# Hybrid RWKV-7 and attention layer: 64-byte buffer lines, score start tied to q and k, and a reordered recurrent build

## Chip, cores and metric

The program runs on one core of a Trainium2 chip. The metric is the device time of one execution in microseconds (us), given as the median of three runs; a profile of one execution goes with it. The engines are TensorE (PE, with its weight loads as PEld), VectorE (DVE), ScalarE (ACT), GpSimd (POOL) and SyncE (SP), which here only issues DMAs.

## What is computed

One layer on 512 tokens of width 2048 in fp32, with 16 attention heads and 16 RWKV-7 heads of 64 columns each:

```python
h = rms_norm(x, norm_g)
q, k, v, z_att, u_shift, z_rwkv = split(h @ w_in)     # one combined projection
att = dilated_mixture_attention(q, k, v, pos) * silu(z_att)
rwk = rwkv7_time_mix(u_shift, z_rwkv, ...)            # token shift, loras, recurrence, group norm, gate
x = x + concat([att, rwk]) @ w_out
return rms_norm(x, final_g)
```

The recurrence runs over the 512 tokens with a 64x64 state per head: `state = state*w + (state@a) b^T + v k^T`, `y = state @ r`. Attention is causal, and mixes three dilations by their softmax denominators.

## The kernel before

**Tiling.** Activations lie with 128 features on the partitions and 512 tokens along the free axis. A weight chunk is loaded as `raw` (512 KB), split by ScalarE and VectorE into a high and a low fp32r part (`whi`, `wlo`), and each product is made of three fp32r matmuls (`hh` with `whi`, `hl` with `whi`, `hh` with `wlo`). One output tile of the input projection takes 48 matmuls of 512 columns into a PSUM tile `mm_*` of pool `pm`. `run_main` writes this main stream tile by tile: `lora`, then `k`, `r`, `v` of the eight RWKV head pairs with the attention gates `z0` to `z7` between them, `gl128`, `qk00` to `qk33` (four groups g of four heads; a group has two head pairs, so pair = 2g or 2g+1), `v` of the attention, the RWKV gates `z8` to `z15`, and at the end the output projection (`mo`, `mh`, `mt`).

**Order.** The program is scheduled by hand. Everything that is not the main stream is a generator (`pre`, `subst`, `merges`, `build`, `scan` of the recurrent part; `assemble`, `att` of the attention; `gate_g`). After each matmul `pump()` resumes those whose turn has come by a small cost model (`Model`, `Engine`, `Tensor`, `Queue`): a `yield 0.1, t` says "resume 0.1 us after tile t is ready by the model". So a wait written in a generator moves where its instructions stand in every engine's queue; the engines themselves then work in order, and wait on semaphores for what they really need. The model knows reads and writes by tile name. It does not know when a buffer of a pool is taken over by a new tile: that wait is put in by the build.

**Pools.** `k2` has 20 buffers of up to 520 columns, `k4` has 9 of 1024 columns (four hold `vt` for the whole attention), `ps` in PSUM has 4. Tiles take them in turn.

**Attention.** `assemble(g, j, ...)` gathers q (j=0) and k (j=1) of a pair by eight DMAs each on SP (`qa_*`, `ka_*`, from the rotated tiles `m0_*`, `m2_*`), and makes `q`, `kd` and `kl` from them. `att(g)` runs over units (pair, block t of 128 queries): scores `s{pair}{head}{t}` (one matmul with `kd`, one with `kl`), masked maximum into `ss`, exp on ScalarE with its sum `den`; one unit later the transposes `pt` into `pa` (k4) and `pb` (k2); two units later, at t = 3, the product `po{pair}` with `vt`, and `yl{pair}` (the gate, fetched by DMA from `sp_s`) times `po`.

**RWKV gates.** `gate(idx, z_ps)` makes `zz`, `zt` (k2) and the gated `yl` from the main stream's tile; `gate_g(p)` makes `pg{p}` from `gh`, `gl`.

**Recurrent part.** `pre(p)` builds for pair p the operands of the blocked recurrence: `pM`, then `pb` (bonus), `L`, `FT` (from `pF`), `X`, `pQ`, and transposed blocks of `bt` and `v` into `X` and `A`. `L` is one buffer for all pairs, and so `pre(p)` waits there until pair p-1 is built.

Of the kernel before, what the change touches and what calls it, by code (L numbers as in the profile page):

```python
# [136 lines left out]
def hymba_kernel(ctx: ExitStack, tc: tile.TileContext, xT, x, wa, wb, wo, pv, w2a2, g2, fg,  # L137
# [20 lines left out]
    K1N, K2N, K4N, RAWN, AHEAD = 5, 20, 9, 2, 2  # L158

    def k2(shape, name, dt=F32):  # L160
        return kp.tile(shape, dt, tag="k2", bufs=K2N, name=name)

    def k1(shape, name, dt=F32):
        return kp.tile(shape, dt, tag="k1", bufs=K1N, name=name)
# [1 line left out]
    def k4(shape, name, dt=F32):  # L166
        return kp.tile(shape, dt, tag="k4", bufs=K4N, name=name)

    def ps(name, shape=(P, 512)):
        return pp.tile(list(shape), F32, tag="ps", name=name)  # L170

    def small(shape, name, bufs=12, dt=F32):
        return sp.tile(shape, dt, tag=f"s{shape[1]}", bufs=4 if shape[1] == 4 else bufs, name=name)

    pvt = cp.tile([P, NPV], F32, name="pvt")
    nc.scalar.dma_start(pvt, pv)

    def col(n, i):
        return pvt[:, PV[n] + i:PV[n] + i + 1]
# [7 lines left out]
    ones = k2([P, P], "ones")  # L187
    V.memset(ones, 1.0)
    bonesr = cp.tile([P, P], F32R, name="bonesr")
    hw0 = cp.tile([P, 16], F32, name="hw0")  # L190
    nka = cp.tile([P, 8], F32, name="nka")
    omu = cp.tile([P, 27], F32, name="omu")
    V.tensor_scalar(omu, pvt[:, 0:27], -1.0, 1.0, ALU.mult, ALU.add)
    warm = cp.tile([P, 1], F32, name="warm")
    S.activation(warm, ones[:, 0:1], AF.Tanh)

    hth, htl, normed = [], [], []
    rstd = cp.tile([P, T], F32, name="rstd")
    rtok = cp.tile([P, 4], F32, name="rtok")
    xt_b, xq_b, Lb = [], [], []  # L200

    def prologue():
# [52 lines left out]
    def later():  # L255
        bones = k2([P, P], "bones")
        Q.dma_start(bones, cst[:, 576:704])
        Q.dma_start(bmt, bmask)
        yield 1.59, bones
        V.tensor_copy(bonesr, bones)  # L260
        V.tensor_scalar(hw0, pvt[:, PV["w0"]:PV["w0"] + 16], 0.5, None, ALU.mult)
        V.tensor_scalar(nka, pvt[:, PV["k_a"]:PV["k_a"] + 8], -1.0, None, ALU.mult)
        for i in range(2):
            G.memset(xt_b[i], 0.0)
            G.tensor_copy(Lb[i][H[i], :, H[i]], ident[H[i], H[i]][:, None, :].to_broadcast([64, NCH, C]))
            yield 0.5, G
# [320 lines left out]
    def c3(t):  # L587
        return t.rearrange("p (c t) -> p c t", t=C)
# [38 lines left out]
    def pre(p, r, k, v):  # L627
# [80 lines left out]
        V.tensor_scalar(rn2, rn2, 1e-24, None, ALU.max)  # L708
        V.reciprocal(rn2, rn2)
        start(subst(p, Mp, rn2), 0.06, Mp, rn2, rank=-1)  # L710
        S.activation(a, a, AF.Identity, bias=nka[:, p:p + 1], scale=col("k_a", p))
        V.scalar_tensor_tensor(k, a, 1.0, k, ALU.add, ALU.mult)
        rk = k2([P, T], f"rk{p}")
        V.scalar_tensor_tensor(rk, r, col("r_k", p), k, ALU.mult, ALU.mult)
# [9 lines left out]
        V.tensor_tensor(bn, pb, v, ALU.mult)  # L724
        yield 0.1, bn
        spill_out(f"bn{p}", bn)
        while p >= 1 and p - 1 not in built:
            yield 0.5
        L = Lb
        X = [k4([P, NCH, P], f"X{h}_{p}") for h in range(2)]  # L730
        for h in range(2):
            S.copy(X[h][H[h], :, H[h]], ident[H[h], H[h]][:, None, :].to_broadcast([64, NCH, C]))
            evac(L[h][H[h], :, H[1 - h]], c3(k)[H[h]])
            evac(X[h][H[h], :, H[1 - h]], c3(r)[H[h]])
        yield 0.1, L[0], L[1]
        FT = k4([P, NCH, P], f"FT{p}")
        for q in range(2):
            pF = ps(f"pF{p}{q}", (P, 4, P))
            for c4 in range(4):
                c = 4 * q + c4  # L740
                for h in range(2):
                    TE.matmul(pF[H[h], c4, :], Fa[H[h], c, :], L[h][H[h], c, :], start=True, stop=True)
            V.tensor_tensor(FT[:, 4 * q:4 * q + 4, :], pF, fmask[:, None, :].to_broadcast([P, 4, P]), ALU.mult)
            yield 0.3
        yield 0.1, X[0], X[1]
        pQ = ps(f"pQ{p}", (P, NCH, C))
        for c in range(NCH):
# [8 lines left out]
        yield from blocks(lambda h: A[h], v, True, f"zv{p}")  # L756
        for h in range(2):
            G.memset(A[h][H[h], 0, :], 0.0)
        state[p] = dict(X=X, L=L, FT=FT, A=A, xt=xt_b[p % 2], wc=wc)
        yield 0.5  # L760

    def subst(p, Mp, rn2):
        V.tensor_tensor(Mp, Mp, rn2[:, None, :].to_broadcast([P, 32, 32]), ALU.mult)
# [266 lines left out]
    def att(g):  # L1030
        units = [(2 * g + pr_, t) for pr_ in range(2) for t in range(4)]
        po, ssb_, pts = {}, {}, {}
        for u in range(len(units) + 2):
            if u < len(units):
                pair, t = units[u]
                while pair not in ready or (t == 0 and u == 0 and pair >= 2 and pair - 1 not in scored):
                    yield 0.5
                tl_ = pairs[pair]
                n = max(256, 128 * (t + 1))
                nv = 128 * (t + 1)  # L1040
                tsl = slice(t * P, (t + 1) * P)
                for h in range(2):
                    sc = ps(f"s{pair}{h}{t}")
                    TE.matmul(sc[:, 0:n], tl_["q"][:, h, tsl], tl_["k", h][:, 0:n], start=True, stop=False)
                    TE.matmul(sc[:, 0:n], tl_["q"][:, h, tsl], tl_["kl", h][:, 0:n], start=False, stop=True)
                    ss = k2([P, T], f"ss{pair}{h}{t}")
                    nm = small([P, 1], f"nm{pair}{h}{t}")
                    V.tensor_tensor_reduce(ss[:, 0:nv], sc[:, 0:nv], att_mask(t), -0.125, 3.0e38,
                                           ALU.add, ALU.min, accum_out=nm)
                    den = small([P, 1], f"den{pair}{h}{t}")  # L1050
                    S.activation(ss[:, 0:nv], ss[:, 0:nv], AF.Exp, bias=nm, scale=-1.0, accum_out=den)
                    ssb_[u, h] = (ss, den)
                if t == 3:
                    scored.add(pair)
            if u >= 2:
                pair, t = units[u - 2]
                if t == 3:
                    po[pair] = pm.tile([P, T], F32, tag="mm", name=f"po{pair}")
                    for j in range(4):
                        for h in range(2):  # L1060
                            hd = (2 * pair + h) * 64
                            pa, pb = pts[pair, h]
                            pj = (pa[:, 0:512], pa[:, 512:896], pb[:, 0:256], pb[:, 256:384])[j]
                            TE.matmul(po[pair][H[h], j * P:T], vt[j][:, hd:hd + 64], pj,
                                      start=(j == 0), stop=(j == 3))
                if t == 3:
                    if f"s{pair}" in spill:
                        o = yl.pop(pair)
                        V.tensor_tensor(o, o, po.pop(pair), ALU.mult)
                    else:  # L1070
                        o = k2([P, T], f"o{pair}")
                        S.copy(o, po.pop(pair))
                    spill_out(f"o{pair}", o)
                elif t == 2 and f"s{pair}" in spill:
                    fetch_y(pair, f"s{pair}")
            if 1 <= u <= len(units):
                pair, t = units[u - 1]
                for h in range(2):
                    ss, den = ssb_.pop((u - 1, h))
                    if t == 0:  # L1080
                        pts[pair, h] = (k4([P, 1024], f"pa{pair}{h}"), k2([P, T], f"pb{pair}{h}"))
                    pa, pb = pts[pair, h]
                    pt = ps(f"pt{pair}{h}{t}")
                    for j in range(t + 1):
                        TE.transpose(pt[:, j * P:(j + 1) * P], ss[:, j * P:(j + 1) * P], ident)
                    if t == 0:
                        S.copy(pa[:, 0:P], pt[:, 0:P])
                    else:
                        S.copy(two(pa, t),
                               pt[:, 0:2 * P].rearrange("p (j c) -> p j c", j=2))  # L1090
                    if t >= 2:
                        S.copy(pb[:, (t - 2) * P:(2 * t - 3) * P], pt[:, 2 * P:(t + 1) * P])
            yield 0.0, S
            if u < len(units):
                for h in range(2):
                    ss, den = ssb_[u, h]
                    nv = 128 * (units[u][1] + 1)
                    V.reciprocal(den, den)
                    V.tensor_scalar(ss[:, 0:nv], ss[:, 0:nv], den, None, ALU.mult)
            yield 0.0, V  # L1100
# [324 lines left out]
```

## Time and profile before

| | |
|---|---|
| median of three runs | 1182.05 us (1180.76 to 1182.65) |
| the profiled execution | 1185.02 us |
| its span, first to last instruction | 1182.6 us |
| PE busy | 1149.7 us, 97% of the span |
| PEld busy | 941.8 us |
| DVE, ACT, POOL busy | 742.1, 560.8, 334.1 us |
| mean granted TensorE clock | 0.992 |
| DMA engines' mean busy share | 39.1% for the main queue |

PE is busy nearly all the time, so the time that PE stands idle, and the time in which its clock is at the lower level, is what work on the other engines can give back or cost. The rest of PE's time is matmuls.

### The profile page before, as it was taken

How to read it: one execution, taken by the hardware profiler on the slowest of the kernel's cores; microseconds unless marked ns; L12 is line 12 of the kernel's file. 1: busy time of each engine (PE TensorE's matmuls, PEld its weight loads, DVE VectorE, ACT ScalarE, POOL GpSimd, SP SyncE). 2: the span in 40 equal slices, each digit the busy share in tenths (PEclk: the TensorE clock that was granted, in tenths of full speed). 3: DMA queues.
4: the chain of work that ended last, by engine and by line, in shares of the span. 5: the costliest groups of instructions: out<-in, count | busy, mean ns of one | idle time of the engine just before them, and what ended most of it. 6: DMA issues, size and time to landing. Idle time of an engine off the chain costs nothing. (4 is left out here: it accounts for less than half of the span.)

```text
span 1182.6 us, 19112 instructions
## 1 busy us (share of the span) xinstructions
PE 1149.7 (97%) x6878; PEld 941.8 (80%) x6878; DVE 742.1 (63%) x1522; ACT 560.8 (47%) x1243; POOL 334.1 (28%) x586
## 2 busy tenths in 40 slices
PE   7999999999999999999999999999899999999997
PEld 5877778788778878787799978777777778888897
DVE  5767866868786778778653546465557657243252
ACT  6455444555746655555533345435354445222243
POOL 1005883635627174653640000101010000011020
PEclk9999999999999999999999999999999999999999
DMA  7333342334242424324242354433445336444343
GB/s 260 119 95 114 115 124 73 103 100 121 66 138 72 118 95 125 105 87 111 63 120 61 112 158 132 124 110 107 119 134 148 116 116 215 123 125 130 102 125 143
DMA packets 89870, 139.62 MB, mean 118 GB/s; under 512 B 37936, under 2 KB 47664, under 8 KB 89776
## 3 DMA queue, kind: packets, MB, share of 16 engines
q1 hardware_dynamic: 89344, 137.83, 39.1%
q8 instruction: 54, 0.88, 0.3%
q10 hardware_dynamic: 432, 0.58, 0.1%
q14 instruction: 40, 0.33, 0.1%
HBM read 114.44 MB, written 14.75 MB: 109 GB/s over the span
## 5 line engine op out<-in xcount | busy, mean ns | idle before, releaser
L88 POOL TENSOR_TENSOR Xtmp<-XT,Mp 128x248 f32<-128x248 f32 (+30 forms) x248 | 132.4, 534 | 168.5 <-DVE XT L88 151.1
L88 POOL TENSOR_TENSOR XT<-XT,Xtmp 128x248 f32<-128x248 f32 (+30 forms) x248 | 139.3, 562 | 21.7 <-DVE XT L88 2.1
L121 PE MATMUL mm_qk<-hh,whi 128*128 128x512 f32 x256 | 104.8, 410 | 0.8 <-ACT gtok L88 0.8
L121 PE MATMUL mm_qk<-hl,whi 128*128 128x512 f32 x256 | 104.2, 407 | 0.0
L121 PE MATMUL mm_qk<-hh,wlo 128*128 128x512 f32 x256 | 104.1, 407 | 0.0
L121 PE MATMUL mm_z<-hh,wlo 128*128 128x512 f32 x256 | 103.2, 403 | 0.0
L121 PE MATMUL mm_z<-hl,whi 128*128 128x512 f32 x256 | 103.2, 403 | 0.0
L88 DVE TENSOR_TENSOR wlo<-raw_o,whi 128x512 fp32r<-128x512 f32 x64 | 48.0, 792 | 87.3 <-ACT whi L88 87.3
L121 PE MATMUL mm_z<-hh,whi 128*128 128x512 f32 x256 | 102.7, 401 | 0.0
L88 POOL TENSOR_TENSOR y<-y,fg 128x512 f32<-128x512 f32 (+1 forms) x16 | 19.4, 1244 | 253.5 <-DMA raw_o<-in_wo_dram 156.7
L88 ACT ACTIVATE ss<-ss,nm 128x128 f32<-128x128 f32 (+3 forms) x64 | 35.6, 556 | 105.4 <-DVE nm L88 100.8
L88 ACT ACTIVATE whi<-raw_o 128x512 fp32r<-128x512 f32 x64 | 36.9, 623 | 96.3 <-PE mo L121 73.4
L88 POOL TENSOR_TENSOR m<-m,m 128x512 f32<-128x512 f32 x16 | 22.2, 1410 | 213.4 <-DVE m L88 127.7
L121 PE MATMUL mo<-whi,mh 128*128 128x512 f32 x192 | 75.8, 395 | 0.0
L121 PE MATMUL mo<-whi,ml 128*128 128x512 f32 x192 | 75.8, 395 | 0.0
L121 PE MATMUL mo<-wlo,mh 128*128 128x512 f32 x192 | 75.8, 395 | 0.0
L88 DVE TENSOR_TENSOR wlo<-raw_v,whi 128x352 fp32r<-128x352 f32 (+1 forms) x80 | 49.5, 640 | 33.8 <-ACT whi L88 33.0
L88 DVE TENSOR_TENSOR wlo<-raw_qk,whi 128x512 fp32r<-128x512 f32 x64 | 45.0, 716 | 31.8 <-ACT whi L88 31.7
L121 PE MATMUL mv<-whi,hh 128*128 128x352 f32 x192 | 62.5, 326 | 1.1 <-DVE m L88 1.1
L121 PE MATMUL mv<-whi,hl 128*128 128x352 f32 x192 | 62.4, 325 | 0.0
L121 PE MATMUL mv<-wlo,hh 128*128 128x352 f32 x192 | 62.3, 324 | 0.0
L88 ACT ACTIVATE whi<-raw_v 128x352 fp32r<-128x352 f32 (+1 forms) x80 | 41.3, 543 | 38.8 <-PE mv L121 25.8
(304 smaller groups left out, 3033.9 us busy)
## 6 DMA issues: line engine op xcount, KB each, us to landing
raw_z<-in_wa_dram SPq DMA_DIRECT2D x32, 512.0 KB
raw_qk<-in_wa_dram SPq DMA_DIRECT2D x32, 512.0 KB
raw_o<-in_wo_dram SPq DMA_DIRECT2D x32, 512.0 KB
raw_v<-in_wb_dram SPq DMA_DIRECT2D x24, 352.0 KB
raw_r<-in_wa_dram SPq DMA_DIRECT2D x16, 512.0 KB
raw_v<-in_wa_dram SPq DMA_DIRECT2D x16, 512.0 KB
raw_k<-in_wa_dram SPq DMA_DIRECT2D x15, 512.0 KB
xk<-in_xT_dram SPq DMA_DIRECT2D x16, 256.0 KB
```

Of the source, the lines that this page charges most:

```text
L88: return fn(o, *args, **kw)
L121: return fn(o, lhs, rhs, **kw)
```

## The change

Four things change. (1) Buffers: every `k2` tile is now a slice of a 528-column buffer (2112 bytes, a multiple of 64) instead of up to 520 columns (2080 bytes, which alternates between 0 and 32 past a 64-byte line); a few constant tiles are enlarged or merged (`nka` becomes columns 16 to 23 of `hw0`). (2) `att` waits at t = 0 by the model until `q` and both `kl` of the pair are written before it issues the pair's first scores. (3) In `pre`, `X`, `pQ` and the transposed blocks come first, and the wait for pair p-1 stands only ahead of `L` and `FT`. (4) `pre` ends with a wait for `FT` of 0.1 in place of a plain 0.5. No step of the arithmetic is changed.

```diff
--- before.py
+++ after.py
@@ -158,7 +158,9 @@
     K1N, K2N, K4N, RAWN, AHEAD = 5, 20, 9, 2, 2
 
     def k2(shape, name, dt=F32):
-        return kp.tile(shape, dt, tag="k2", bufs=K2N, name=name)
+        t = kp.tile([P, 528], dt, tag="k2", bufs=K2N, name=name)
+        t = t[:, 0:math.prod(shape[1:])]
+        return t if len(shape) == 2 else t.rearrange("p (a b) -> p a b", b=shape[2])
 
     def k1(shape, name, dt=F32):
         return kp.tile(shape, dt, tag="k1", bufs=K1N, name=name)
@@ -172,8 +174,8 @@
     def small(shape, name, bufs=12, dt=F32):
         return sp.tile(shape, dt, tag=f"s{shape[1]}", bufs=4 if shape[1] == 4 else bufs, name=name)
 
-    pvt = cp.tile([P, NPV], F32, name="pvt")
-    nc.scalar.dma_start(pvt, pv)
+    pvt = cp.tile([P, 112], F32, name="pvt")
+    nc.scalar.dma_start(pvt[:, 0:NPV], pv)
 
     def col(n, i):
         return pvt[:, PV[n] + i:PV[n] + i + 1]
@@ -187,16 +189,15 @@
     ones = k2([P, P], "ones")
     V.memset(ones, 1.0)
     bonesr = cp.tile([P, P], F32R, name="bonesr")
-    hw0 = cp.tile([P, 16], F32, name="hw0")
-    nka = cp.tile([P, 8], F32, name="nka")
+    hw0 = cp.tile([P, 32], F32, name="hw0")
     omu = cp.tile([P, 27], F32, name="omu")
     V.tensor_scalar(omu, pvt[:, 0:27], -1.0, 1.0, ALU.mult, ALU.add)
-    warm = cp.tile([P, 1], F32, name="warm")
+    warm = small([P, 1], "warm")
     S.activation(warm, ones[:, 0:1], AF.Tanh)
 
     hth, htl, normed = [], [], []
     rstd = cp.tile([P, T], F32, name="rstd")
-    rtok = cp.tile([P, 4], F32, name="rtok")
+    rtok = cp.tile([P, 16], F32, name="rtok")[:, 0:4]
     xt_b, xq_b, Lb = [], [], []
 
     def prologue():
@@ -258,8 +259,8 @@
         Q.dma_start(bmt, bmask)
         yield 1.59, bones
         V.tensor_copy(bonesr, bones)
-        V.tensor_scalar(hw0, pvt[:, PV["w0"]:PV["w0"] + 16], 0.5, None, ALU.mult)
-        V.tensor_scalar(nka, pvt[:, PV["k_a"]:PV["k_a"] + 8], -1.0, None, ALU.mult)
+        V.tensor_scalar(hw0[:, 0:16], pvt[:, PV["w0"]:PV["w0"] + 16], 0.5, None, ALU.mult)
+        V.tensor_scalar(hw0[:, 16:24], pvt[:, PV["k_a"]:PV["k_a"] + 8], -1.0, None, ALU.mult)
         for i in range(2):
             G.memset(xt_b[i], 0.0)
             G.tensor_copy(Lb[i][H[i], :, H[i]], ident[H[i], H[i]][:, None, :].to_broadcast([64, NCH, C]))
@@ -708,7 +709,7 @@
         V.tensor_scalar(rn2, rn2, 1e-24, None, ALU.max)
         V.reciprocal(rn2, rn2)
         start(subst(p, Mp, rn2), 0.06, Mp, rn2, rank=-1)
-        S.activation(a, a, AF.Identity, bias=nka[:, p:p + 1], scale=col("k_a", p))
+        S.activation(a, a, AF.Identity, bias=hw0[:, 16 + p:17 + p], scale=col("k_a", p))
         V.scalar_tensor_tensor(k, a, 1.0, k, ALU.add, ALU.mult)
         rk = k2([P, T], f"rk{p}")
         V.scalar_tensor_tensor(rk, r, col("r_k", p), k, ALU.mult, ALU.mult)
@@ -724,24 +725,10 @@
         V.tensor_tensor(bn, pb, v, ALU.mult)
         yield 0.1, bn
         spill_out(f"bn{p}", bn)
-        while p >= 1 and p - 1 not in built:
-            yield 0.5
-        L = Lb
         X = [k4([P, NCH, P], f"X{h}_{p}") for h in range(2)]
         for h in range(2):
             S.copy(X[h][H[h], :, H[h]], ident[H[h], H[h]][:, None, :].to_broadcast([64, NCH, C]))
-            evac(L[h][H[h], :, H[1 - h]], c3(k)[H[h]])
             evac(X[h][H[h], :, H[1 - h]], c3(r)[H[h]])
-        yield 0.1, L[0], L[1]
-        FT = k4([P, NCH, P], f"FT{p}")
-        for q in range(2):
-            pF = ps(f"pF{p}{q}", (P, 4, P))
-            for c4 in range(4):
-                c = 4 * q + c4
-                for h in range(2):
-                    TE.matmul(pF[H[h], c4, :], Fa[H[h], c, :], L[h][H[h], c, :], start=True, stop=True)
-            V.tensor_tensor(FT[:, 4 * q:4 * q + 4, :], pF, fmask[:, None, :].to_broadcast([P, 4, P]), ALU.mult)
-            yield 0.3
         yield 0.1, X[0], X[1]
         pQ = ps(f"pQ{p}", (P, NCH, C))
         for c in range(NCH):
@@ -756,8 +743,24 @@
         yield from blocks(lambda h: A[h], v, True, f"zv{p}")
         for h in range(2):
             G.memset(A[h][H[h], 0, :], 0.0)
+        while p >= 1 and p - 1 not in built:
+            yield 0.5
+        L = Lb
+        for h in range(2):
+            evac(L[h][H[h], :, H[1 - h]], c3(k)[H[h]])
+        yield 0.1, L[0], L[1]
+        FT = k4([P, NCH, P], f"FT{p}")
+        for q in range(2):
+            pF = ps(f"pF{p}{q}", (P, 4, P))
+            for c4 in range(4):
+                c = 4 * q + c4
+                for h in range(2):
+                    TE.matmul(pF[H[h], c4, :], Fa[H[h], c, :], L[h][H[h], c, :], start=True, stop=True)
+            V.tensor_tensor(FT[:, 4 * q:4 * q + 4, :], pF, fmask[:, None, :].to_broadcast([P, 4, P]), ALU.mult)
+            yield 0.3
         state[p] = dict(X=X, L=L, FT=FT, A=A, xt=xt_b[p % 2], wc=wc)
-        yield 0.5
+        yield 0.1, FT
+
 
     def subst(p, Mp, rn2):
         V.tensor_tensor(Mp, Mp, rn2[:, None, :].to_broadcast([P, 32, 32]), ALU.mult)
@@ -1036,6 +1039,8 @@
                 while pair not in ready or (t == 0 and u == 0 and pair >= 2 and pair - 1 not in scored):
                     yield 0.5
                 tl_ = pairs[pair]
+                if t == 0:
+                    yield 0.1, tl_["q"], tl_["kl", 0], tl_["kl", 1]
                 n = max(256, 128 * (t + 1))
                 nv = 128 * (t + 1)
                 tsl = slice(t * P, (t + 1) * P)
@@ -1171,7 +1176,7 @@
             yield 1.05
 
     fgt = []
-    ssq = cp.tile([P, 4, 5], F32, name="ssq")
+    ssq = cp.tile([P, 4, 8], F32, name="ssq")
     yt = {}
 
     def residual(nb):
```

The order of instructions shifts in the whole program from these waits. Three places, each with its queue before and after.

**VectorE at the start of pair 2** (first scores `s200`). Before, `kl_100` stands behind the product of `yl1` with `po1`:

```order
L88 TENSOR_TENSOR yl1_7964<-yl1_7964,po1_7994 128x512 [waits DMAHW6_49,PE_49,Pool_49]
L88 TENSOR_TENSOR m0_20_8012<-mm_qk20_7830,L0_234 128x512 [waits PE_49]
L88 TENSOR_TENSOR m3_20_8014<-mm_qk20_7830,L0_234 128x512
L88 TENSOR_TENSOR q_11_8016<-qa_110_7923,q_11_8016 64x512 [waits DMAHW1_49,DMAHW0_49,Activation_49]
L88 TENSOR_TENSOR q_11_8016<-qa_111_7928,q_11_8016 64x512 [waits DMAHW3_49,DMAHW2_49,Activation_49]
L88 TENSOR_TENSOR wlo112_8026<-raw112_qk22_7886,whi112_8025 128x512 [waits DMAHW5_49,Activation_49]
L88 TENSOR_TENSOR wlo112_8026<-raw112_qk22_7886,whi112_8025 128x512 [waits Activation_49]
L88 TENSOR_TENSOR kl_100_8047<-ka_100_7933,kd_100_8046 128x512 [waits DMAHW1_49,DMAHW7_49,DMAHW0_49,Activation_49]
L88 TENSOR_TENSOR kl_101_8051<-ka_101_7938,kd_101_8050 128x512 [waits DMAHW4_49,DMAHW3_49,DMAHW5_49,DMAHW2_49,Activation_49]
L88 ISA ss200_8062,nm200_8063<-s200_8059,L1_237 128x128 [waits PE_49]
```

After:

```order
L88 TENSOR_TENSOR kl_100_7976<-ka_100_7893,kd_100_7975 128x512 [waits DMAHW6_49,DMAHW1_49,DMAHW7_49,DMAHW0_49,Activation_49]
L88 TENSOR_TENSOR kl_101_7980<-ka_101_7898,kd_101_7979 128x512 [waits DMAHW4_49,DMAHW3_49,DMAHW5_49,DMAHW2_49,Activation_49]
L88 TENSOR_TENSOR m0_20_8001<-mm_qk20_7825,L0_233 128x512 [waits PE_49]
L88 TENSOR_TENSOR m3_20_8003<-mm_qk20_7825,L0_233 128x512 [waits PE_49]
L88 TENSOR_TENSOR wlo112_8010<-raw112_qk22_7881,whi112_8009 128x512 [waits Activation_49]
L88 TENSOR_TENSOR q_11_8032<-qa_110_7946,q_11_8032 64x512 [waits DMAHW1_49,DMAHW0_49,Activation_49]
L88 TENSOR_TENSOR q_11_8032<-qa_111_7951,q_11_8032 64x512 [waits DMAHW3_49,DMAHW2_49,Activation_49]
L88 TENSOR_TENSOR wlo112_8010<-raw112_qk22_7881,whi112_8009 128x512 [waits Activation_49]
L88 ISA ss200_8051,nm200_8052<-s200_8048,L1_236 128x128 [waits PE_49]
```

`kl_100` and `kl_101` moved ahead of the product with `po1`, which now stands six rows behind `ss200`; on TensorE `s200` stands 17 rows ahead of `po1`'s first row, where it stood 35 rows behind it. For pair 4, `s400` still follows `po3`, with 41 matmuls of `qk30` and `qk31` between them instead of 27; for pair 0, `s000` follows 11 matmuls later in the main stream; for pair 6, `s600` moved from behind `po5` to ahead of it.

**VectorE at the end of pair 5** (`ss503` is the fourth block of head 0 of pair 5, which the transposes `pt503` need). Before:

```order
L88 RECIPROCAL den513_9170<-den513_9170 128x1
L88 TENSOR_SCALAR ss513_9167<-ss513_9167,den513_9170 128x512 [waits DVE_49]
L88 TENSOR_TENSOR wlo127_9224<-raw127_z9_9059,whi127_9223 128x512 [waits DMAHW4_49,PE_49,Activation_49]
L88 TENSOR_TENSOR wlo127_9224<-raw127_z9_9059,whi127_9223 128x512 [waits Activation_49]
L88 TENSOR_TENSOR gl1_9125<-gw1_9118,gh1_9124 128x128 [waits DMAHW3_49,PE_49,Activation_49]
L88 TENSOR_TENSOR gl1_9125<-gw1_9118,gh1_9124 64x128 [waits DMAHW7_49,DMAHW6_49]
L88 TENSOR_TENSOR yl8_9116<-yl8_9116,pg0_9263 128x512 [waits DMAHW2_49,Pool_49]
L88 TENSOR_TENSOR q_31_9272<-qa_310_9187,q_31_9272 64x512 [waits DMAHW5_49,DMAHW4_49,Activation_49]
L88 TENSOR_TENSOR q_31_9272<-qa_311_9192,q_31_9272 64x512 [waits DMAHW7_49,DMAHW6_49,Activation_49]
L88 TENSOR_TENSOR zz8_9293<-mm_z8_9074,rstd_93 128x512 [waits PE_49]
L88 SCALAR_TENSOR_TENSOR zt8_9295<-zt8_9295,zz8_9293 128x512 [waits Activation_49]
L88 SCALAR_TENSOR_TENSOR yl8_9116<-zt8_9295,yl8_9116 128x512 [waits DVE_49]
```

After:

```order
L88 ISA ss610_9289,nm610_9290<-s610_9286,L1_236 128x128 [waits DMAHW5_49,DMAHW3_49,DMAHW7_49,DMAHW1_49,PE_49]
L88 ISA nm610_9290 128x1
L88 TENSOR_TENSOR zz8_9307<-mm_z8_9031,rstd_92 128x512 [waits DMAHW5_49,DMAHW7_49,DMAHW3_49,DMAHW1_49]
L88 SCALAR_TENSOR_TENSOR zt8_9309<-zt8_9309,zz8_9307 128x512 [waits DMAHW4_49,DMAHW2_49,DMAHW6_49,DMAHW0_49,Activation_49]
L88 SCALAR_TENSOR_TENSOR yl8_9041<-zt8_9309,yl8_9041 128x512 [waits DVE_49]
L88 TENSOR_TENSOR wlo128_9318<-raw128_z10_9117,whi128_9317 128x512 [waits Activation_49]
L88 RECIPROCAL den503_9230<-den503_9230 128x1
L88 TENSOR_SCALAR ss503_9227<-ss503_9227,den503_9230 128x512 [waits DVE_49]
L88 RECIPROCAL den513_9238<-den513_9238 128x1
L88 TENSOR_SCALAR ss513_9235<-ss513_9235,den513_9238 128x512 [waits DVE_49]
```

Before, `zz8` stands behind the two blocks of pair 5 and waits for TensorE. Now it stands ahead of them and waits for four DMA queues: it takes the buffer of `m0_31`, which the DMAs `ka_310` and `ka_311` read, and `zt8` takes that of `m2_31`. These eight DMAs stand on SP behind the eight of `qa_310` and `qa_311`, the first of which waits for `s513`. On TensorE the stretch from `s513` to `pt503` holds, after six transposes, 40 matmuls of `z8` and `z9` and the four of `s600` and `s610` (256 columns); it held 22 matmuls.

**ScalarE at the start of pair 6** (`pa61` takes the first block of head 1 of pair 6). Before:

```order
L88 ACTIVATE whi129_9377<-raw129_z10_9238 128x512
L88 ACTIVATE ss601_9423,den601_9426<-ss601_9423,nm601_9424 128x256 [waits DVE_49]
L88 ACTIVATE ss611_9431,den611_9434<-ss611_9431,nm611_9432 128x256 [waits DVE_49,Activation_49]
L88 COPY pa60_9436<-pt600_9438 128x128 [waits PE_49]
L88 COPY pa61_9441<-pt610_9443 128x128 [waits PE_49]
L88 ACTIVATE zt9_9458<-zz9_9456 128x512 [waits DVE_49,Activation_49,Pool_49]
```

After:

```order
L88 ACTIVATE ss601_9390,den601_9393<-ss601_9390,nm601_9391 128x256 [waits DVE_49,Activation_49]
L88 ACTIVATE ss611_9398,den611_9401<-ss611_9398,nm611_9399 128x256 [waits DVE_49]
L88 COPY pa60_9403<-pt600_9405 128x128 [waits PE_49]
L88 COPY pa61_9408<-pt610_9410 128x128 [waits PE_49,Activation_49]
L88 ACTIVATE whi129_9362<-raw129_z10_9213 128x512
L88 ACTIVATE kd_310_9421<-ka_310_9267 128x512 [waits DMAHW5_49,DMAHW3_49]
L88 ACTIVATE kd_311_9425<-ka_311_9272 128x512 [waits DMAHW7_49,DMAHW1_49]
L88 ACTIVATE zt9_9457<-zz9_9455 128x512 [waits DVE_49,PE_49,Activation_49]
```

`pa61` takes the `k4` buffer of `pa50`, which `po5` reads. Before it stood behind `po5`; now `pt610` and `pa61` come 39 rows of TensorE ahead of it, and the build has it wait for the third matmul of `po5`. `whi129` (the second half), both `kd`, `zt9` and the split of chunk 130 stand behind it, and on VectorE `wlo129` stands behind `whi129`.

## Rows read from the trace of the kernel before

**Rows 1.** Waits of TensorE, whole span: total us, times, longest.

```profile
PE s L121 <- DVE kl L88: 6.4, 3, 3.5
...
PE zpb L121 <- DVE xnb L88: 1.8, 2, 1.2
PE pb L121 <- DVE l_rk L88: 1.5, 2, 1.0
PE s L121 <- ACT kd L88: 1.3, 1, 1.3
```

**Rows 2.** Timeline, 768 to 776: start, us, instruction, [idle before and its releaser].

```profile
768.15 0.69 DVE L88 TENSOR_TENSOR yl<-yl,po 128x512 f32<-128x512 f32 x1 [6.50 <-DMA yl<-sp_s]
...
772.61 1.28 DVE L88 TENSOR_TENSOR kl<-ka,kd 128x512 fp32r<-128x512 f32 x2
...
773.34 0.39 PE L121 MATMUL s<-kl,q 128*128 128x256 f32 x1 [2.48 <-DVE kl L88]
...
775.30 0.63 PE L121 MATMUL mm_qk<-hl,whi 128*128 128x512 f32 x1
...
775.72 0.63 PE L121 MATMUL mm_qk<-hh,wlo 128*128 128x512 f32 x1
```

**Rows 3.** Timeline of TensorE, 834 to 839.

```profile
834.45 0.28 PE L121 MATMUL s<-kd,q 128*128 128x256 f32 x1
...
838.22 0.38 PE L121 MATMUL s<-kl,q 128*128 128x256 f32 x1 [3.49 <-DVE kl L88]
```

**Rows 4.** Windows: stretch, length, busy us of each engine, granted clock, DMA.

```profile
772.00:780.00 8.00, 6.56 (x24) 5.28 (x25) 4.55 (x15) 2.03 (x6) 0.00 (x0) 0.79 0.60 145
```

**Rows 5.** Timelines: pair 4's k DMAs and kd; pair 6's and 7's DMAs.

```profile
827.79 2.22 SPq L133 DMA_DIRECT2D ka<-m  x2
...
831.51 0.63 ACT L88 ACTIVATE kd<-ka 128x512 fp32r<-128x512 f32 x1 [0.96 <-DMA ka<-m]
...
883.95 5.30 SPq L133 DMA_DIRECT2D qa<-m  x8
889.34 4.96 SPq L133 DMA_DIRECT2D ka<-m  x8
```

**Rows 6.** Timelines of VectorE and ScalarE, 887 to 898.

```profile
887.50 0.16 DVE L88 RECIPROCAL den<-den 128x1 f32<-128x1 f32 x1
887.70 0.49 DVE L88 TENSOR_SCALAR ss<-ss,den 128x512 f32<-128x512 f32 x1
...
894.97 0.63 ACT L88 ACTIVATE zt<-zz 128x512 f32<-128x512 f32 x1 [1.55 <-DVE zz L88]
...
895.64 0.69 DVE L88 SCALAR_TENSOR_TENSOR zt<-zt,zz 128x512 f32<-128x512 f32 x1 [0.70 <-ACT zt L88]
...
896.97 1.29 DVE L88 TENSOR_TENSOR wlo<-raw_z,whi 128x512 fp32r<-128x512 f32 x2
```

**Rows 7.** Timeline of TensorE, 882 to 902.

```profile
882.97 0.82 PE L121 MATMUL pt<-csts,ss 128*128 128x128 f32 x6
...
883.87 0.40 PE L121 MATMUL mm_z<-hh,wlo 128*128 128x512 f32 x1
...
888.53 0.40 PE L121 MATMUL mm_z<-hl,whi 128*128 128x512 f32 x1
...
898.81 1.72 PE L121 MATMUL po<-pa,vt 128*64 128x512 f32 x8
...
901.12 0.50 PE L121 MATMUL mm_z<-hh,whi 128*128 128x512 f32 x1
```

**Rows 8.** Waits of TensorE, 876 to 1000 (the one row there is).

```profile
PE pg L121 <- DVE nm L88: 0.2, 1, 0.2
```

**Rows 9.** Groups by shape: duration in ns (min/median/max), first and last start.

```profile
L121 PE MATMUL mm_z<-hh,whi x256: 387/396/503, 95.8 to 993.7; 128*128 128x512 f32 x128
...
L121 PE MATMUL mo<-whi,mh x192: 393/396/397, 994.4 to 1128.1; 128*128 128x512 f32 x192
...
L88 DVE TENSOR_TENSOR zz<-mm_z,rstd x16: 647/684/692, 109.5 to 994.6; 128x512 f32<-128x512 f32 x16
```

## The prediction

> **What bounds the kernel now.** I read the waits of TensorE first, since TensorE is busy for 97% of the span. Summed over the whole program its idle time is small, and its largest single entry is the first-score matmul `s`, which waits for VectorE's `kl` three times (6.4 us) and for ScalarE's `kd` once (1.3) [rows 1]. Next I read the timeline at these places. At the start of pair 2 TensorE stands 2.48 us because `kl` starts only at 772.61; VectorE had been held until 768.15 by the product `yl<-yl,po`, whose fetched factor came 6.50 us late, and worked through its queue from there [rows 2]. Pair 4 repeats it with 3.49 us [rows 3]. Pair 0 is the third. A second loss hangs on each: after it a step of the main stream takes 0.42 us (775.30 to 775.72) [rows 2] where it takes (888.53-883.87)/20 = 0.233 [rows 7], and the granted clock of the eight microseconds around it is 0.79 [rows 4]. So the clock falls to its lower level of 1.2 GHz after each of these gaps and each costs 0.21 x 8 = 1.7 us more; the row stands for three that read alike. From 876 to 1000, the stage of pairs 6 and 7 and the RWKV gates, TensorE waits 0.2 us in all [rows 8]. That is the stage that I expect to lose.
>
> **What the score wait removes.** 7.7 us of waiting [rows 1] and 3 x 1.7 = 5.1 us of low clock are at stake. For pairs 0 and 2 the scores come 11 matmuls later, or with `kl` ahead of the late product; both stalls should vanish. For pair 4 the product with `po3` still stands ahead, so `kl` is no earlier; the scores come 14 matmuls later, 14 x 0.233 = 3.3 us of a wait that ran from 834.57 to 838.22 (the `kd` half at 834.45, 0.12 long at this rate). About 0.4 us stays, too short a gap beside the others to lower the clock. Gain: 7.7 - 0.4 + 5.1 = 12.4 us. What is late next: the masked maxima of those scores, and with them the transposes; by the order these have 13 matmuls or more of cover (3.0 us), against about 1.3 us of split work that now stands ahead of `ss400`. I cost it at nothing.
>
> **What it adds: VectorE's wait at `zz8`.** Scores of pair 6 are now issued before pair 7's q and k are gathered, and `zz8` and `zt8` fall on the buffers that pair 7's eight k DMAs read. SP issues 16 DMAs back to back from the end of `s513`: 5.30 + 4.96 in the rows, 10.35 us from the first's start to the last's end [rows 5]. The last lands 1.5 us after its issue ends (830.01 to 831.51, a `kd` that waited for its DMA) [rows 5]. So `zt8` on ScalarE starts 11.85 us after `s513`. From there to a finished `ss503` it is 2.0 us to the start of `wlo` (894.97 to 896.97), 0.65 for one `wlo`, 0.20 and 0.49 for the reciprocal and the scaling [rows 6]: 3.3. `pt503` can start 15.2 us after `s513`. TensorE gets there in 0.58 (six transposes: 0.90 to the second matmul behind them, less one step and the change of form) + 40 x 0.233 + 4 x 0.12 = 10.4 us [rows 7]. Stall: 4.8, and 0.2 more at `pt513`; 5.0 us, and 1.7 of low clock, since the gap is twice that of pair 2. With issues at 0.5 us each the stall would be 2.9; with a landing later by the same distance longer than I take, some 6.5.
>
> **What it adds: ScalarE's wait at `pa61`.** `pa61` waits for the third of `po5`'s eight matmuls, about 1.2 us into a `po` that takes 2.31 (898.81 to 901.12) [rows 7]. ScalarE then does the copy and half a split (0.4 and 0.63, the second as `zt` in [rows 6]); VectorE follows with `wlo129` (0.65), two `kl` (1.3), two scalings (some 1.1), `zz9`, `zt9` and `yl9` (2.7 with ScalarE's part), two `wlo130` (1.3), `gl2` in two pieces (0.6), `yl5` (0.65), `wlo131` (0.65), `ss602` (0.5). All but the small pieces are full tiles at the spacing of [rows 6]. `ss602` frees the PSUM buffer that `pg2` needs: 11.7 us after `po5` begins. TensorE stands there after 2.31 + 9 x 0.233 + four scores of 384 columns (0.7) + transposes (0.4) = 5.5, plus about 0.8 of waiting at `pt601`. Stall: 0.8 + 5.4, taken as 6.0 with some overlap, and 1.7 of low clock. If `gl2` alone bound it, 4; nothing excludes 7.
>
> **The smaller parts.** In the recurrent part the same kind of wait comes up at `g128l`, VectorE's second factor of the gate lora: it takes the buffer that `pa7` reads and stands 35 matmuls (8.2 us) ahead of it. Behind it VectorE has about 11.7 us of work up to `bt7`, and TensorE 46 matmuls and 16 small ones, also 11.7: 0.5 us, bounds 0 and 3. The reorder itself lets X, Q and blocks run earlier, but the waits that it could shorten are a few (`zpb` 1.8, `pb` 1.5 [rows 1]); I take half, a gain of 1.6, and as bounds all of it and a loss as large. Buffers on 64-byte lines: `zz` runs in buffers of both kinds and its 16 durations lie within 647 to 692 ns; `mm_z` has its weights 32 past a line and its activations on one, `mo` the reverse, and both take 396 ns [rows 9]. I cost it at nothing. The Trainium skill (SBUF — State Buffer, Operand start alignment) asks only that an operand start at a multiple of its element size, and says that this is legality and was not timed; by that too the term is nothing.
>
> **Sum.** -12.4 + (5.0 + 1.7) + (6.0 + 1.7) + 0.5 - 1.6 = +0.9 us on the profiled execution of 1185.0, which lies 3.0 above the median of the runs: 1182.05 + 0.9 = 1183.0. A measurement of this kernel tells about 0.2% (2.4 us) from no change, so the forecast is a tie: what the three score stalls give back is paid again one stage later.
>
> **Rivals.** (a) *The new waits are covered, the gain stays.* It needs the last k DMA to land within 10.4 - 3.3 = 7.1 us of `s513`, 16 issues at 0.35 us; or `pg2`'s buffer to come free within 6.3 us of `po5`. The rows speak against the first (0.65 and 0.62 per issue [rows 5]), and the second rests on my count of VectorE's queue. One of the two gone: 1183.0 - 7 = 1176; both: 1169. Chance 0.27. (b) *Slower: `pM7` starves.* If VectorE needs its full 0.69 per tile instead of 0.65 and the queue behind `g128l` grows by a few rows, `bt7` is late by up to 3 us and the low clock adds 1.7: +4.2 beyond my 0.5, 1187. It decides as soon as VectorE's work there exceeds TensorE's 11.7 us by more than 1. Chance 0.1. (c) *The lines matter after all.* Only matmuls with both operands on a line are not in the trace. At the low clock a step takes 0.42 [rows 2], half of which is 0.212, yet at the high clock it takes 0.233: something holds it by 0.02. If that were the alignment, 3,360 matmuls of 512 columns (58 input tiles of 48, 576 of `mo`) would give back 70 us: 1113. But `mm_z` and `mo` each have one operand on a line and lose the same, so I give it 0.05. The Trainium skill (TensorE: Matmul & The Clock Gate, Wait — 56ns, not 53.3ns?) puts the step at 512/2.4 + 2.5 ns, an estimate of 216 ns here; the trace's 233 does not agree, which is why this rival stays. (d) *The scores still wait*, because `kl` comes late all the same: 1183 + 12 = 1195, chance 0.03.
>
> **How the numbers follow.** The forecast has 0.55; its own range is 1179 to 1188 from the bounds above. Of its chance I put 0.27 within 0.2% of 1182.05, 0.23 above and 0.05 below. Faster: 0.05 + 0.27 + 0.05 = 0.37; slower: 0.23 + 0.1 + 0.03 = 0.36; same 0.27. The range runs from between the two cases of (a) to above (b): 1172 to 1190. Left out are both waits gone, (c) and (d).
>
> **What would show it.** No row `s <- kl` above 0.5 us, and no clock of 0.79 at the starts of pairs 0, 2 and 4. In their place a wait of `pt` for VectorE's `ss` of about 5 us at the end of pair 5, with VectorE idle for `ka` DMAs ahead of `zz`; one of `pg` of about 5 us in `z10`, with ScalarE idle for `po` ahead of a `pa`; a lower clock after each. Matmul steps at 0.233 as before. I am wrong if these two waits are missing or much shorter, or if steps change.

## The result and the profile after

The changed kernel takes 1187.57 us (median of five runs, 1185.99 to 1189.14) where the kernel before took 1182.05: ratio 1.0051, 95% interval 1.0037 to 1.0065. It is slower by 5.5 us; the forecast was 1183.0. The two profiled executions differ by less, 1185.99 to 1185.02, since the one of before lies 3.0 above its median and the one of after 1.6 below its own. So sizes below come from the medians, places from the traces. One execution each of two kernels below, the changed kernel 64 bytes further (2245.67 us) and the better version (3920.09, the one that was profiled), took far longer than the rest: the ratios leave them out, the medians do not, and no step is read from that trace.

TensorE's waits in the changed kernel (total us, times, longest), to hold against [rows 1]:

```profile
PE pt L121 <- DVE den L88: 5.4, 3, 3.7
PE pg L121 <- DVE nm L88: 5.0, 1, 5.0
PE zpb L121 <- DVE xnb L88: 2.7, 2, 1.7
PE mm_k L121 <- DVE u_lora L88: 1.6, 1, 1.6
...
PE s L121 <- DVE kl L88: 1.0, 2, 0.7
```

The scores' 7.7 us have become 1.0; `pt`, which had no row before, and `pg`, which had 0.2, bring 10.4. Windows by stage of the changed kernel (stretch, length, busy us of PE, PEld, DVE, ACT, POOL with counts, granted clock, DMA share, GB/s):

```profile
690.00:876.00 186.00, 183.64 (x895) 145.86 (x894) 117.14 (x299) 89.44 (x242) 17.07 (x12) 1.00 0.44 130
876.00:1000.00 124.00, 113.64 (x522) 89.26 (x521) 69.31 (x162) 50.46 (x132) 0.00 (x0) 0.94 0.43 131
```

The same view of the kernel before:

```profile
690.00:876.00 186.00, 178.00 (x848) 140.59 (x849) 108.12 (x282) 85.16 (x230) 13.71 (x10) 0.97 0.42 123
876.00:1000.00 124.00, 123.84 (x590) 98.36 (x589) 79.98 (x183) 57.99 (x151) 3.01 (x2) 1.00 0.52 154
```

The stage of the first scores gained 5.6 us of TensorE's work and its full clock; the next stage, which had waited 0.2 us [rows 8], lost 10.2 and clock. The timeline of the changed kernel shows both new waits:

```profile
876.60 0.40 PE L121 MATMUL s<-kl,q 128*128 128x512 f32 x1
...
877.02 3.04 SPq L133 DMA_DIRECT2D qa<-m  x5
...
878.05 0.55 PE L121 MATMUL pt<-csts,ss 128*128 128x128 f32 x3 [0.73 <-DVE yl L88]
...
882.07 4.96 SPq L133 DMA_DIRECT2D ka<-m  x8
...
887.81 0.69 DVE L88 TENSOR_TENSOR zz<-mm_z,rstd 128x512 f32<-128x512 f32 x1 [4.67 <-DMA ka<-m]
...
891.50 0.49 DVE L88 TENSOR_SCALAR ss<-ss,den 128x512 f32<-128x512 f32 x1
...
892.13 1.09 PE L121 MATMUL pt<-csts,ss 128*128 128x128 f32 x4 [3.73 <-DVE den L88]
...
896.43 0.63 PE L121 MATMUL mm_z<-hl,whi 128*128 128x512 f32 x1
896.86 0.56 PE L121 MATMUL mm_z<-hh,wlo 128*128 128x512 f32 x1
897.26 0.39 PE L121 MATMUL mm_z<-hh,whi 128*128 128x512 f32 x1
...
905.48 1.73 PE L121 MATMUL po<-pa,vt 128*64 128x512 f32 x8
...
907.29 0.27 ACT L88 COPY pa<-pt 128x128 f32<-128x128 f32 x1 [9.61 <-PE po L121]
...
908.12 0.69 DVE L88 TENSOR_TENSOR wlo<-raw_z,whi 128x512 fp32r<-128x512 f32 x1 [11.43 <-ACT whi L88]
...
910.62 0.87 PE L121 MATMUL pt<-csts,ss 128*128 128x128 f32 x4 [0.72 <-DVE den L88]
...
916.70 0.55 DVE L88 CUSTOM_DVE_ANT_0 ss<-s,L 128x384 f32<-128x384 f32 x1
...
917.40 0.76 PE L121 MATMUL pg<-g128h,gh 128*128 128x512 f32 x1 [4.98 <-DVE nm L88]
...
921.26 0.39 PE L121 MATMUL mm_z<-hl,whi 128*128 128x512 f32 x1
```

`s513` ends at 877.00, and SP's sixteen DMAs of pair 7 start with it. VectorE stands 4.67 us at `zz8` for the k DMAs that read its buffer, and the transposes of the block of pair 5 behind it come 15.1 us after `s513`'s end. ScalarE stands 9.61 us at `pa61` for `po5`, VectorE 11.43 behind it, and `pg2` comes 11.9 us after `po5`'s start. After each gap TensorE works on at its lower level, 1.2 GHz: a step (from the start of one matmul of the main stream to the start of the next) is still 0.43 at 896.43 and 0.23 from 897.26; after the second gap it is short again from 921.26.

### The profile page after: what moved, and what is told of

Read it like the earlier page. It is cut to its first block, busy times and chain, and to the rows that moved or that the text cites. A ratio compares the mean times of both kernels' runs of the same rounds, so it can differ in the third digit from the quotient of the medians.

```text
span 1183.9 us, 19123 instructions
## 1 busy us (share of the span) xinstructions
PE 1146.4 (97%) x6878; PEld 938.2 (79%) x6878; DVE 735.2 (62%) x1511; ACT 568.6 (48%) x1254; POOL 336.4 (28%) x586
## 5 line engine op out<-in xcount | busy, mean ns | idle before, releaser
L88 POOL TENSOR_TENSOR Xtmp<-XT,Mp 128x248 f32<-128x248 f32 (+30 forms) x248 | 128.9, 520 | 143.6 <-DVE XT L88 112.8
L88 POOL TENSOR_TENSOR XT<-XT,Xtmp 128x248 f32<-128x248 f32 (+30 forms) x248 | 144.6, 583 | 21.4 <-DVE XT L88 2.5
L121 PE MATMUL mm_qk<-hh,whi 128*128 128x512 f32 x256 | 102.2, 399 | 0.8 <-ACT gtok L88 0.8
L88 DVE TENSOR_TENSOR wlo<-raw_z,whi 128x512 fp32r<-128x512 f32 x64 | 48.1, 771 | 33.2 <-ACT whi L88 32.9
```

Of the source, the lines that this page charges most:

```text
L88: return fn(o, *args, **kw)
L121: return fn(o, lhs, rhs, **kw)
```

## The experiments

All medians of five rounds beside the kernel before (1181.7 to 1181.9 there), intervals 95%.

**One part at a time.** The change's first part alone (all buffer hunks of the diff):

```diff
-        return kp.tile(shape, dt, tag="k2", bufs=K2N, name=name)
+        t = kp.tile([P, 528], dt, tag="k2", bufs=K2N, name=name)
...
-    hw0 = cp.tile([P, 16], F32, name="hw0")
-    nka = cp.tile([P, 8], F32, name="nka")
+    hw0 = cp.tile([P, 32], F32, name="hw0")
```

> Only the buffer sizes and merged constants of the change, on the kernel before. Theory A (the loss of the changed kernel comes from two waits for buffers in the stage of pairs 5 to 7, both caused by the score wait): no more than 2 us from before, the three score stalls stay, no wait of pt or pg above 1 us from 876 to 1000. Rival B (the lines or the reorder cost the time in the first 690 us): 3 us or more slower than before. Rival C (lines make matmuls or tile operations faster): steps of the main stream below 0.233 us and a clear gain.

Measured 1189.78, ratio 1.0077 (1.0059 to 1.0094). The term that I costed at nothing costs 8 us by itself: rival B in size, though theory A's signs hold (the score stalls stay, and there is no new wait of `pt` or `pg`).

The recurrent part's new sequence alone (the hunks of `pre`):

> Only the reorder in the recurrent build (and its last wait) on the kernel before. Theory A: within 2 us of before, the score stalls as before; waits of the recurrent part (zpb, pb, pM, pF, Y) change by no more than 2 us in all. Rival B: 3 us or more slower.

Measured 1178.46, 0.9972 (0.9963 to 0.9982): a gain of 3.3, more than theory A allowed and the other way from rival B. Of the waits in [rows 1] `pb`'s 1.5 is gone and `zpb`'s 1.8 is 0.3; `Y`, which had waited 0.8 in all, waits more:

```profile
PE Y L121 <- DVE A L88: 1.8, 2, 1.1
PE Y L121 <- ACT A L88: 1.7, 4, 0.7
...
PE zpb L121 <- DVE xnb L88: 0.3, 1, 0.3
```

The score wait alone:

```diff
                 tl_ = pairs[pair]
+                if t == 0:
+                    yield 0.1, tl_["q"], tl_["kl", 0], tl_["kl", 1]
```

> Only the score wait on the kernel before. Theory A: all of the loss is here: the stalls at pairs 0, 2 and 4 go (about 5.6 us of idle time and three dips of the clock, 5.1), the waits at pt503 and pg2 come (about 10 us and 6.9 of low clock), 1186 to 1190. Rival B: a gain of 5 us or more, since without lines and reorder the two new waits would be all there is.

Measured 1185.92, 1.0038 (1.0026 to 1.005): a loss of 4.2, by theory A at its lower end. Its TensorE waits from 690 to 1000 are the changed kernel's:

```profile
PE pt L121 <- DVE den L88: 5.7, 3, 3.8
PE pg L121 <- DVE nm L88: 5.0, 1, 5.0
PE pt L121 <- DVE yl L88: 0.9, 2, 0.7
PE s L121 <- DVE kl L88: 0.6, 1, 0.6
```

**Which pairs.** The changed kernel with the wait for pairs 0 and 2 only:

```diff
-                if t == 0:
+                if t == 0 and pair in (0, 2):
```

> The changed kernel with the score wait for pairs 0 and 2 only. By the order of the built program the order of stage 5 to 7 goes back to that of before, zz8 and pa61 no longer wait for k DMAs and po5, and the stall at pair 4 is back. Theory A: two stalls and two dips of the clock gone (4.2 + 3.4 us), none new: 1173 to 1177. Rival B: 1180 or more, because the loss is not in that stage.

Measured 1177.48, 0.9963 (0.9951 to 0.9975), half a microsecond above theory A. The one long score wait that is left is the one at pair 4, the wait of `pg` is gone, and `pt` waits 1.0 in all:

```profile
PE s L121 <- DVE kl L88: 4.0, 2, 3.6
...
PE pt L121 <- DVE den L88: 1.0, 1, 1.0
```

So the wait at pairs 0 and 2 removes two stalls and brings only this 1.0 us at `pt`. The wait at the other pairs saves 3.6 us and its low clock at pair 4 and costs both new waits: 10.1 us net. Pair 4 and pair 6 were not run apart.

**The two new waits, taken out of the changed kernel.** First `zz8` and `zt8` out of the shared buffers (a recurrence tile that is idle by then, and the tile's own PSUM), TensorE's order unchanged:

```diff
+        if idx == 8:
+            z, th = xt_b[1].rearrange("p c t -> p (c t)"), z_ps
```

> The changed kernel with zz8 in a tile that is free by then and zt8 in the PSUM tile it is made from; order of TensorE unchanged, so VectorE no longer waits there for the k DMAs of pair 7. Theory A: the wait at pt503 (4.4 us with its neighbours) and its 3.4 us of low clock go, 1179 to 1181; the wait of pg for 5 us stays. Rival B (the wait only moves to the next instruction that needs the DMAs, or the two waits hide one another): 1185 to 1188.

Measured 1181.14, 0.9994 (0.9985 to 1.0002): 6.4 us back. From 876 to 1000 the `pt` wait is down to 0.7, `pg` as before:

```profile
PE pg L121 <- DVE nm L88: 5.0, 1, 5.0
PE pt L121 <- DVE yl L88: 0.9, 2, 0.7
PE pt L121 <- DVE den L88: 0.7, 1, 0.7
```

Then `zz9` and `zt9` as well, and pair 6's first transposes behind `po5`:

```diff
+                while u == 1 and g == 3 and pair - 1 not in summed:
+                    yield 0.5
```

> The changed kernel without either wait: zz8, zt8, zz9, zt9 as in the run before this, and the first transposes of pair 6 issued behind po5, so that pa61 finds its buffer free. Theory A: some 17 us below the changed kernel (10.3 of waits, 6.9 of low clock), 1169 to 1173, TensorE's waits from 876 to 1000 below 2 us. Rival B: 1178 or more, since later scores then wait in turn.

Measured 1171.84, 0.9922 (0.9909 to 0.9935): another 9.3. The one wait that is left from 876 to 1000:

```profile
PE pt L121 <- DVE yl L88: 0.7, 1, 0.7
```

Both together cost 15.7 us.

**What is in the buffer part.** The sizes of the first part, with `nka` in a tile of its own and, beyond the change, two more constants enlarged (`omu` and `warm`), so that the weight chunks do not lie where the change has them; no row of any queue differs from the kernel before:

```diff
-    nka = cp.tile([P, 8], F32, name="nka")
+    nka = cp.tile([P, 16], F32, name="nka")[:, 0:8]
```

> The kernel before with every buffer on 64-byte lines, and nothing else: hw0 and nka stay two tiles, so the order of instructions is that of before on every engine. Theory A (the 8 us that the part with the lines costs come from the order, which moves because two constants share a tile): within 1.5 us of before, all steps and waits as before. Rival B (the place of the buffers itself costs): 4 to 10 us slower. Rival C: faster by more than 2 us.

Measured 1173.47, 0.9932 (0.9919 to 0.9944): 8.2 us faster (rival C), where the part with the merge is 8.1 slower. Two rows of its timeline with nineteen main-stream steps between them:

```profile
875.60 0.40 PE L121 MATMUL mm_z<-hh,wlo 128*128 128x512 f32 x1
...
879.96 0.39 PE L121 MATMUL mm_z<-hh,whi 128*128 128x512 f32 x1
```

4.36/19 = 0.2295 a step at a granted clock of 1.00, where the kernel before has 0.233 [rows 7]. The merge alone, in a tile as long as the two, so that nothing moves in memory:

```diff
-    hw0 = cp.tile([P, 16], F32, name="hw0")
-    nka = cp.tile([P, 8], F32, name="nka")
+    hw0 = cp.tile([P, 24], F32, name="hw0")
```

> The kernel before with nka put into hw0 alone, in a tile as long as the two together, so that no address behind it moves. Theory A (the two constants in one tile shift the model's first waits and with them the order, and this costs what the sizes run with the merge lost): 1181.7 + 8.1 + 2.3 (what the weights' place gave back there, 0.6 ns x 2,784 and 0.5) = about 1192, with longer waits of TensorE in the recurrent part. Theory B (the loss there came from addresses): as before, 1181 to 1183.

Measured 1192.63, 1.0093 (1.008 to 1.0106), by theory A. Its TensorE waits:

```profile
PE Y L121 <- DVE A L88: 2.9, 2, 2.5
PE gp L121 <- ACT L L88: 2.5, 2, 2.1
PE gp L121 <- DVE L L88: 2.5, 1, 2.5
...
PE mm_k L121 <- DVE u_lora L88: 1.6, 1, 1.6
```

Before, `Y` waits 0.8, `mm_k` for `u_lora` 0.2, and `gp` not at all. The order of every engine differs from the first pairs on, because the model knows tiles by name and the two constants now share one. The first part of the change has this very order on every engine, so the two runs differ by the sizes alone: 1189.78 to 1192.63, which makes the sizes worth about -2.9.

**Which bytes.** The kernel before with one constant 32 bytes longer, so that the weight chunks move and the `k2` buffers still alternate:

```diff
-    ssq = cp.tile([P, 4, 5], F32, name="ssq")
+    ssq = cp.tile([P, 4, 8], F32, name="ssq")
```

> The kernel before with one constant (ssq) 32 bytes longer, so that everything placed behind it lies 32 bytes further and the weight chunks start at 64 past a multiple of 128 bytes instead of 32; k2 buffers still alternate between 0 and 32 past a 64-byte line, and the order of every queue is as before. Theory A (the place of the weight chunks sets the matmul step: 233.2 ns a step at 32 past 128, 232.6 at 0 in the changed kernel, 229.4 at 64 in the sizes-only run): step 229.4 ns, 2,784 of them, so about 8 to 10 us less, 1172 to 1174. Theory B (the k2 buffers on lines made the gain of the sizes-only run): step 233.2, time as before, 1181 to 1183.

Measured 1179.56, 0.998 (0.9971 to 0.9989): neither. Ten main-stream steps of it:

```profile
887.63 0.39 PE L121 MATMUL mm_z<-hh,whi 128*128 128x512 f32 x1
...
889.96 0.39 PE L121 MATMUL mm_z<-hl,whi 128*128 128x512 f32 x1
```

2.33/10 = 0.233, as before. And the changed kernel with its first constant 64 bytes longer:

```diff
-    pvt = cp.tile([P, 112], F32, name="pvt")
+    pvt = cp.tile([P, 128], F32, name="pvt")
```

> The changed kernel with its first constant 64 bytes longer, order of every queue as in the changed kernel, all k2 buffers still on 64-byte lines, the weight chunks at 64 past a multiple of 128 instead of 0. Theory A (place of the weight chunks): step 232.6 falls to 229.4, 3.1 ns x 2,784 = 8.6, and 1 to 2 in the last products: 1187.6 - 10 = about 1177. Theory B (a 64-byte line is all that counts): as the changed kernel, 1186 to 1189.

Measured 1181.02, 0.9995 (0.9984 to 1.0006), 6.6 less than the changed kernel, by two thirds theory A. Fourteen steps of it:

```profile
896.71 0.39 PE L121 MATMUL mm_z<-hh,wlo 128*128 128x512 f32 x1
...
899.91 0.39 PE L121 MATMUL mm_z<-hl,whi 128*128 128x512 f32 x1
```

3.20/14 = 0.2286. By the build's addresses, with the mean of all steps below 300 ns in each trace (`mm`: input projection, `mo`: output):

| kernel | weight chunks, bytes past a multiple of 256 | `mm` step, ns | `mo` step, ns |
|---|---|---|---|
| before | 160 | 233.2 | 233.3 |
| changed | 0 | 232.6 | 232.4 |
| sizes alone | 64 | 229.5 | 233.3 |
| changed, 64 bytes further | 64 | 229.7 | 233.3 |
| before, 32 bytes further | 192 | 233.2 | 228.9 |
| the better version below, 32 bytes further | 192 | 233.2 | 233.3 |

The step follows the place of the weight chunks, but by 256 bytes and not, as my theory had it, by 128: 64 helps, 192 does not. The `mm` steps of the other traces fall in with it: 232.6 in four more kernels at 0, 233.2 to 233.3 in three more at 160. The `k2` lines alone do not make it (the second and fourth rows have them alike); 64 without them was not run. In `mm` the weight chunk is the operand that is loaded into TensorE, in `mo` it is the one that streams through, and `mo` does not follow the place: at 0 it is 232.4 in three kernels and 233.3 in two.

**A better version.** The kernel before with the reorder and the score wait, both new waits taken out as above, without the buffer part:

> The reorder and the score wait on the kernel before (hw0 and nka as before), with both new waits taken away as in the run before this. Theory A, if the parts add up: 1181.8 - 3.3 (reorder alone) - 10 to 11 (the three score stalls with their clock) = 1167 to 1169. Rival B: no better than the run with the wait for pairs 0 and 2 only, 1177, if the reorder's gain and the score wait's do not add.

Measured 1168.66, 0.989 (0.9874 to 0.9906), by theory A. With `ssq` 32 bytes longer:

> The kernel before with the reordered recurrent build, the score wait, zz8, zz9 and their tanh tiles taken out of the shared buffers, pair 6's first transposes behind pair 5's product, and ssq 32 bytes longer; its order is that of the same kernel without the longer constant (1168.7). Theory A: 8 to 10 us less than that, 1159 to 1161. Theory B: 1167 to 1170.

Measured 1169.01, 0.9897 (0.9883 to 0.9912): theory B, as the table's last row explains for the main stream. The place at 64 past 256 was not tried on it.

## Why the prediction was right where it was, and wrong where not

**The range held, the tie did not.** 1187.57 lies in 1172 to 1190. The forecast was a tie and gave 0.36 to slower; the loss is 5.5, which this measurement can tell. Two agreements are luck. Between the two profiled executions the difference is +1.0, the sum's +0.9, though the score part alone makes +3.8 there by the rows below, and the rest, which I had too small or at nothing, brings it down. And rival (b)'s 1187 is the measured time, but its mechanism did not come: VectorE does stand 4.06 us at `g128l` for `pa7` (until 522.81), yet `pM7` behind it, at 535.8, waits for nothing.

**The score waits: right but for one link.** From 7.7 us to 1.0, with the clock at 1.00 through the stage. I had left 0.4 at pair 4, where 0.66 came. The transposes behind the later scores, which I costed at nothing, wait at pair 0:

```profile
708.53 0.70 PE L121 MATMUL pt<-csts,ss 128*128 128x128 f32 x2 [0.92 <-DVE den L88]
```

**The wait at `zz8`: right on VectorE, off by 1.0 on TensorE.** 15.2 us from `s513` to the transposes were forecast, 15.1 came. TensorE arrived 11.4 after it instead of 10.4, 0.73 of it by a wait of its own for `yl` (878.05), so the stall was 3.7 instead of 5.0. Taken out, it gives back 6.4 where 6.7 were forecast. One figure beside it is a slip: with issues at 0.5 us the same sum gives about 2.6, not 2.9; nothing rested on it.

**The wait at `pa61`: right.** 6.0 forecast; 0.72 + 4.98 = 5.7 came, and `pg2` 11.9 us after `po5`'s start instead of 11.7. Taken out together with the smaller waits, it gives back 9.3 where 7.7 were forecast. Rival (a), covered waits, falls with both.

**The low clock after them: too small.** I took 1.7 us each from [rows 4]. After the gap in [rows 2], which ends at 773.34, TensorE first runs at the high level; the timeline of the kernel before shows the change of length at 774.87:

```profile
774.39 0.39 PE L121 MATMUL mm_qk<-hl,whi 128*128 128x512 f32 x1
774.62 0.46 PE L121 MATMUL mm_qk<-hh,wlo 128*128 128x512 f32 x1
774.87 0.63 PE L121 MATMUL mm_qk<-hh,whi 128*128 128x512 f32 x1
```

After the two new gaps it is at the low level from the first instruction, to about 897.2 and 921.1. At half speed these 5.0 and 3.7 us cost 2.5 and 1.9, an estimate from those rows. With `yl`'s 0.9 and pair 0's 0.9 at `pt` the score part comes to -(7.7 - 1.0 + 5.1) + 3.7 + 5.7 + 4.4 + 0.9 + 0.9 = +3.8 where I had +2.0; measured alone it is +4.2.

**The low clock of the three score stalls: true of the profiled execution, too much for the median.** I took 3 x 1.7 us from a trace with a mean clock of 0.992 and added the sum to the median. Of the 22 executions of the kernel before that stand beside the last four runs, the three at 0.992 took 1183.7 to 1184.1 us, the other nineteen, at 0.993 to 0.996, 1180.5 to 1182.6. The kernel before 32 bytes further, with the same queues, shows the case: pair 2 stalls as long as in [rows 2], and the window that has a clock of 0.79 in [rows 4] has 1.00 here:

```profile
771.72 0.39 PE L121 MATMUL s<-kl,q 128*128 128x256 f32 x1 [2.53 <-DVE kl L88]
...
772.00:780.00 8.00, 7.90 (x39) 6.43 (x39) 5.51 (x21) 3.44 (x12) 0.20 (x1) 1.00 0.73 197
```

So a gap of the same length costs low clock in one execution and none in another. What the median execution had of the 5.1 us was not measured; the less it had, the less the score wait could give back.

**The reorder: mis-sized.** -1.6 forecast, -3.3 measured alone; the +0.5 of TensorE behind `g128l` did not come. I had taken half of the waits that it could shorten; alone it takes 3.0 of these 3.3 and pays part of it back at `Y`, and the smaller waits of `pM` (1.0) and `mv` (1.1) go with them.

**"Buffers on 64-byte lines: I cost it at nothing": wrong, twice over.** This is the step that failed. In the change's company the part is worth 5.5 - 4.2 + 3.3 = +4.6 us, if the parts add up; measured with both new waits taken out, it is +3.2 (1171.84 with it, 1168.66 without). It holds two effects of opposite sign that I had not looked for. One is no matter of bytes: the merge of two constants moves the order of every queue, +10.7 alone. Some of it survives in the changed kernel (`mm_k` for `u_lora` 1.6, as in the merge alone, and `zpb` 2.7, where the reorder alone had 0.3); the waits of `gp` for `L` do not. With the sizes at -2.9 the +3.2 leaves about 6 of the merge's 10.7, an estimate; whether the reorder or the score wait undoes the rest was not run apart. The other effect is rival (c) in a small form. I argued from [rows 9] that a matmul's time does not depend on its operands' lines, but those durations, all near 396 ns, do not carry the step: matmuls overlap, and what counts is start to start. There the places that I compared differ by 0.1 ns, and another place gives 3.7 less: 2,784 x 3.7 ns = 10.3 us, of which 8.2 showed; `zpb`, `pb` and `pM` wait 6.9 us in that trace where they waited 5.0. The change itself has its weights at 0 past 256 and gets 0.6 ns of it, 1.7 us. The Trainium skill (SBUF — State Buffer, Operand start alignment) leaves open what a start address costs in time, and so gave no ground for a term of nothing; here it costs up to 1.6% of a matmul step. The Trainium skill's 216 ns for a step (TensorE: Matmul & The Clock Gate, Wait — 56ns, not 53.3ns?) is reached at none of the places.

**What stays open.** Why 64 past 256 is the better place: the other operands (`hh`, `hl`, `mh`, `ml`) lie at 128 past 256 in all kernels, and no run moved them. Why the output projection ran at 228.9 in one trace and at 233.3 in another with the same places:

```profile
1040.00 0.39 PE L121 MATMUL mo<-whi,mh 128*128 128x512 f32 x1
...
1045.95 0.39 PE L121 MATMUL mo<-whi,ml 128*128 128x512 f32 x1
```

is the kernel before 32 bytes further, 26 steps of 0.2288; the best version 32 bytes further has 25 of 0.2332:

```profile
1040.02 0.40 PE L121 MATMUL mo<-whi,ml 128*128 128x512 f32 x1
...
1045.85 0.40 PE L121 MATMUL mo<-whi,mh 128*128 128x512 f32 x1
```

If the first is the rule for that kernel, 576 x 4.4 ns = 2.5 us is all of its gain of 2.4.

## What to carry to other kernels

Issuing work earlier moves buffers earlier: before a wait is removed, list what the moved instructions take over and which transfers still read it, since a pool's next tile can cost a stage later what the first stage gained. Where a model keyed by names sets the order, an edit of names or tiles is an edit of the schedule, and is compared queue by queue before it is costed at nothing. Read a matmul's cost from start to start, and try the weights' address as a parameter of its own.

## What was not expected of the hardware

A step of 512 columns at the granted clock of 1.00 of the input projection takes 229.5 and 229.7 ns in the two kernels with the weight chunks at 64 past a multiple of 256 bytes, and 232.6 to 233.3 in the eleven others traced, at 0, 160 and 192. The length of a gap of TensorE did not settle what the clock did after it. A gap of 2.48 us was followed by 1.5 us at the high level and then by the low one (773.34 to 774.87); one of 2.53 us, at the same place in the kernel before 32 bytes further, by a clock of 1.00. After 3.73 us the work of the changed kernel starts at the low level and stays there for five microseconds (clock 0.59 from 889 to 897); after 3.77 us at the same place, with the score wait alone, it is 0.79 in that window.
